# Two column blocks per bank in the output projections of a fused encoder trunk, and new planner estimates for two of its stages

## The chip, the cores and the metric

The kernel runs as one program on one core of a Trainium2 chip. The metric is the device time of one execution in microseconds (us). Where the profile gives instruction times and waits, they come from one profiled execution of the same program.

## The reference, cut to what matters

The kernel computes two layers of an encoder on one sequence of 256 positions (`S`) with 1024 features. Everything is float32. Each layer is a half feed-forward network, a mixer, a cross-attention to a memory of 256 positions, and another half feed-forward network; every one of them adds its result to `x`.

```python
for layer in range(2):
    x = x + 0.5 * swiglu(rms_norm(x, ...), ...)
    h = rms_norm(x, mix_norm[layer])
    if layer % 2 == 0:      # the "AB" mixer: differential attention | stick-breaking attention
        x = x + concat([from_heads(oa), from_heads(ob)]) @ w_out          # (256 x 1024) @ (1024 x 1024)
    else:                   # the "MLA" mixer: latent attention, 16 heads
        x = x + from_heads(o) @ w_o                                       # (256 x 1024) @ (1024 x 1024)
    x = x + memory_cross_attention(rms_norm(x, ...), rms_norm(mem, ...), ...)
                            # 4 heads of 128; its last step is (256 x 512) @ (512 x 1024)
    x = x + 0.5 * swiglu(rms_norm(x, ...), ...)
```

The three products written out above, the AB one, the MLA one and that of each cross-attention, are the output projections that the change is about. There are four of them in the program.

## The kernel before, in words

`x` is kept transposed: eight blocks of 128 features by 256 positions, called `dt` 0 to 7 here as in the code (d0 to d7 for short). Each product in full precision is made of three matmuls (`mm3`, L285 to L287): high part of the weight with high part of the data, then the low part of the data, then the low part of the weight. L287 is the one that reads the weight's low part in an output projection.

A weight chunk of 2048 columns comes by DMA into a raw buffer `wr` and is split there: ScalarE (ACT) copies it into `wh` (L250), and VectorE (DVE) subtracts that from the raw one into `wl` (L252). In the mixers and cross-attentions this goes in four quarters of 512 columns, and GpSimd (POOL) makes the last quarter of `wl`; in the two small projections of the cross-attentions some chunks go in eight pieces of 256. There are two raw buffers and three pairs of `wh` and `wl` (`HL = 3`). So the fourth chunk in a row can't be split before the last matmul that reads the first chunk.

An output projection is `out_g` (L654 to L684). Its source is in groups: four groups of two rows of 128 features in the mixers, in the order in which attention delivers them. Its weights are `nchunk` chunks, four with two column blocks each in the mixers, two with four blocks each in the cross-attentions. It goes by windows: the first is d0, d1 and d2 together, each with a PSUM bank of its own, group after group; then d3 to d7 come one at a time, with all groups in a row. There are three banks with the tag `mm`.

When a block's last group is done, `finish_dt` handles it. DVE adds the bank to `x` (L511); ACT makes the high part of the scaled block for the next stage (L482), DVE its low part (L483). These three are scheduled with high priority. ACT squares the block (L523), into `acc` for the first and into one of two buffers `sq` for the others, and POOL adds each square to `acc` (L531): seven additions in a row. After the first 48 matmuls of the next stage, TensorE (PE) sums `acc` over the partitions (L476), which starts the next norm.

TensorE's order is fixed by hand. In each stage a small planner (`run`, L438) holds a list of tasks with a priority each, and steps through them by an estimated clock: each step says which events, weights and banks it needs, and the tables `EST_X0`, `EST_X1`, `EST_AB` and `EST_MLA` tell after how many us an event of a task counts as done. The task that is ready, by these estimates, and has the best priority comes next. A weight counts as ready 4.41 us after the buffer it needs comes free. The order on the other engines is set afterwards by the framework's scheduler, from the program order, its own costs and the priorities. On the chip each engine then works its list strictly in that order.

In the AB stage the planner mixes attention with other work: `po` (L1105) is the product of stick-breaking weights and values, scores of the differential attention start at L323 and use two banks `s`, and the values of that part are multiplied at L1191. Beside them stand projections of the memory for the coming cross-attention; the keys of the memory are normalised on DVE (L853) and then transposed on PE (`transpose4`, L793), and `mem_k` is the task that does so, with a latency in its `yield` (L854).

Of the kernel before, what the change touches and what calls it, by code (L numbers as in the profile page):

```python
# [19 lines left out]
P = 128  # L20
S = 256
# [30 lines left out]
BANKS = {"mm": 3, "s": 2, "t": 2, "o": 1}  # L52
# [4 lines left out]
KRAW = True  # L57
PREADD = True

EST_X0 = {'scale': 3.59, 'rq': 1.14, 'psd': 1.46, 'sp': 2.8, 'p1': 4.06, 'p2': 0, 'o': 1.32, 'src': 8.83}  # L60
EST_X1 = {'scale': 2.31, 'rq': 1.14, 'psd': 1.46, 'sp': 2.8, 'p1': 3.39, 'p2': 0.0, 'o': 1.18, 'src': 8.83}
EST_AB = {'b': 1.33, 'va': 1.47, 'rot': 14.92, 'st1': 6.44, 'st2': 0.14, 'z': 1.55, 'sto': 2.4, 'src': 0.79, 'T': 0.74, 'sp': 3.0, 'pc': 8.7, 'pcT': 1.4, 'po': 4.35, 'oa': 8.7, 'srco': 1.25}
PRIO_MLA = [1, 2, 4.2, 3.9, 4.4, 2.3]
PRIO_AB = [1, 6.1, 4.1, 6.9, 6.9, 0.5]
EST_MLA = {'latd': 1.52, 'scale': 11.0, 'r': 1.8, 'kr': 4.06, 'pk': 2.4, 'pv': 1.23, 'v': 1.73, 'k': 6.43, 'kT': 0.9, 'q': 7.82, 'qT': 2.38, 'cs': 3.11, 'sp': 6.25, 'p1': 3.36, 'p2': 0.68, 'p3': 0.75, 'o': 0.58, 'src': 0.8}
# [96 lines left out]
def trunk_kernel(ctx, tc, wflat, xT_d, xtok_d, memT_d, memtok_d, gains_d, rows_d, cst_d, out_d):  # L162
# [57 lines left out]
    offs, o = [], 0  # L220
# [63 lines left out]
    def mm3(out, a, b, first, last, **kw):  # L284
        PE.matmul(out, a[0], b[0], start=first, stop=False, **kw)  # L285
        PE.matmul(out, a[0], b[1], start=False, stop=False, **kw)  # L286
        PE.matmul(out, a[1], b[0], start=False, stop=last, **kw)  # L287
        spend(3 * 0.109 * b[0].shape[-1] / 256)
# [96 lines left out]
    class Event:  # L385
        t = None
# [5 lines left out]
    def spend(n):  # L392
        od.cost += n
# [8 lines left out]
    def drop(ps, dur):  # L402
        tag, i, _ = od.own.pop(id(ps))
        od.pend.append((lambda t, tag=tag, i=i: od.bank[tag].__setitem__(i, t), dur))
# [75 lines left out]
    def split(hi, lo, src, g):  # L480

        return (A.activation(hi, src, AF.Identity, scale=g),  # L482
                V.scalar_tensor_tensor(out=lo, in0=src, scalar=g, in1=hi.bitcast(F32), op0=ALU.mult,  # L483
                                       op1=ALU.subtract))
# [17 lines left out]
    def begin_phase():  # L502
        st.at = x_at.pop(0)
        st.nxt = [None] * KT
        st.acc = None

    def finish_dt(dt, gc, ps=None, factor=1.0):
        xd = x[:, dt, :]
        if ps is not None:
            with tc.high_priority():  # L510
                V.scalar_tensor_tensor(out=xd, in0=ps, scalar=factor, in1=xd, op0=ALU.mult, op1=ALU.add)  # L511
        if gc is None:
            nc.sync.dma_start(out_d[:, dt, :], xd)
            return
        h, l = (z[:, st.at + dt * S:st.at + dt * S + S] for z in parts)
        st.nxt[dt] = (h, l)
        if ps is None:
            return split(h, l, xd, gcol(gc + dt))
        with tc.high_priority():
            split(h, l, xd, gcol(gc + dt))  # L520

        def square(dst):
            A.activation(dst, xd, AF.Square)  # L523

        if st.acc is None:
            st.acc = T("acc", [P, S], 2)
            square(st.acc)
        else:
            sq = T("sq", [P, S], 2)
            square(sq)  # L530
            G.tensor_tensor(out=st.acc, in0=st.acc, in1=sq, op=ALU.add)  # L531
# [121 lines left out]

    def out_g(keyf, nchunk, groups, gc):  # L654

        begin_phase()
        per = KT // nchunk
        ws, left, pss = {}, {c: per for c in range(nchunk)}, {}

        def part(dt, g):  # L660
            _, src, rows_ = groups[g]
            w = ws[dt // per]
            j = dt % per
            for i, k in enumerate(rows_):
                mm3(pss[dt][:, 0:S], (w[0][:, k, j * P:(j + 1) * P], w[1][:, k, j * P:(j + 1) * P]),
                    src[i], g == 0 and i == 0, g == len(groups) - 1 and i == len(rows_) - 1)
            if g == len(groups) - 1:
                left[dt // per] -= 1
                if not left[dt // per]:
                    done(keyf(dt // per))  # L670
                ps = pss.pop(dt)
                finish_dt(dt, gc, ps[:, 0:S])
                drop(ps, 0.8)

        nw = BANKS["mm"]
        for win in [tuple(range(nw))] + [(dt,) for dt in range(nw, KT)]:
            for g, (ev, _, _) in enumerate(groups):
                for dt in win:
                    yield dict(after=[ev], w=keyf(dt // per), mm=int(g == 0))
                    if dt // per not in ws:  # L680
                        ws[dt // per] = weight(keyf(dt // per), per * P)
                    if g == 0:
                        pss[dt] = take("mm")
                    part(dt, g)  # L684

# [149 lines left out]
    def mem_k(l, c, events):  # L835

        ps = yield from tm_g((f"memk{l}", c), memstate["x"])
        rm = memstate["rs"]

        def norm():  # L840
            yield dict(after=events)
            k = al()
            for t in range(2):
                A.activation(k[:, t * S:(t + 1) * S], ps[:, t * S:(t + 1) * S], AF.Identity, scale=rm[:, t:t + 1])
            drop(ps, 1.2)
            sq = al()
            G.tensor_tensor(out=sq, in0=k, in1=k, op=ALU.mult)
            v = sm()[:, 0:4]
            V.tensor_reduce(out=v, in_=sq.rearrange("p (a b) -> p a b", b=P), axis=AX.X, op=ALU.add)
            V.tensor_scalar(out=v, in0=v, scalar1=1.0 / P, scalar2=EPS, op0=ALU.mult, op1=ALU.add)  # L850
            r = rsqrt(v, 4)
            k3 = k.rearrange("p (a b) -> p a b", b=P)
            V.tensor_tensor(out=k3, in0=k3, in1=r.unsqueeze(2).to_broadcast([P, 4, P]), op=ALU.mult)  # L853
            yield dict(t=1, lat=7.0)  # L854
            pt = transpose4([k3[:, t * 2 + j, :] for j in range(2) for t in range(2)])
            kt = al()
            A.activation(kt, pt, AF.Identity, scale=gcol(G_XK + l))
            drop(pt, 0.9)
            rel(k, sq)
            memstate["k", l, c] = kt  # L860

        spawn(1, norm())
# [15 lines left out]
    def cross(l, gc):  # L878
        EST_X = (EST_X0, EST_X1)[l]
        xg = st.xg  # L880
# [89 lines left out]
    def mixer_ab(gc):  # L970
# [12 lines left out]
        def products():  # L983
            for key in ("qb", "kb"):
                for c in range(2):
# [5 lines left out]
                    def evac_b(key=key, c=c, ps=ps):  # L991
# [7 lines left out]
                        drop(ps, 0.9)  # L999
                        signal(ev[key, c], EST_AB['b'])  # L1000

                    spawn(0, after([ev["rb"]], evac_b))
            for key in AB_ORDER:
# [8 lines left out]
                for c in range(2):  # L1012
# [6 lines left out]
                    drop(ps, 1.2)  # L1019
                    signal(ev[key, c], EST_AB['va'])  # L1020
                if dst is None:
# [4 lines left out]
        def rotate(key):  # L1026
# [20 lines left out]
            if key == "qa":  # L1047
                rqs["r"] = r
            signal(ev[key], EST_AB['rot'])

# [9 lines left out]
        def stick(hq, g):  # L1060
# [25 lines left out]
            for i, (z, (sp, hh, hl)) in enumerate(zip(zs, sps)):  # L1086
                yield dict(lat=EST_AB['st2'] if i else EST_AB['st1'])
                for h_ in (hh, hl):
# [5 lines left out]
                strict(w_)  # L1094
                drop(z, EST_AB['z'])
                ws.append(w_)
                rel(sp, hh, hl)
            yield dict(lat=EST_AB['sto'], o=1 - g, after=[ev["vb", hq]] + [ev["po", hq]] * g)
            if g == 0:
# [504 lines left out]
```

## Time and profile before

| what | value |
|---|---|
| device time, median of three runs | 1088.73 us |
| the three runs | 1087.2, 1088.73, 1089.23 us |
| the profiled execution's own time | 1086.18 us |
| its span, first to last instruction | 1084.5 us |
| PE busy | 1063.0 us, 98 % of the span |
| DVE busy | 769.4 us, 71 % |
| ACT busy | 655.3 us, 60 % |
| POOL busy | 192.4 us, 18 % |
| share of PE in the chain that ended last | 90 % |
| HBM read | 190.79 MB |

A busy share is an average over the whole span. The chain that ended last is found backwards from the last instruction, at each step to what released it. The rows that follow further down come from four kinds of view: the page's summary, the sums of waits of an engine, an engine's instructions in order of time, and the busy time and granted TensorE clock of given stretches.

### The profile page before, as it was taken

To read this page: it belongs to the slowest core of one execution; us is meant where nothing else is said; L and a number is where in the kernel's file an instruction comes from. 1 tells how busy PE (TensorE), PEld (TensorE's weight loads), DVE (VectorE), ACT (ScalarE), POOL (GpSimd) and SP (SyncE) were. 2 spreads that over 40 slices of the span, in tenths; PEclk is the share of its full clock that TensorE was granted. 3 is DMA by queue.
4 is the path that set the end of the run, shared out by engine and by line. 5 is a ranking of instruction groups with operands and counts; after the bars stand their busy time and mean duration, and the time that the engine had idled before them with its cause. 6 is when DMAs were issued, how large, how long until landed. Compare 5 with 4: busy or idle time off the path is not lost.

```text
span 1084.5 us, 23380 instructions
## 1 busy us (share of the span) xinstructions
PE 1063.0 (98%) x9034; PEld 1044.5 (96%) x9034; DVE 769.4 (71%) x1866; ACT 655.3 (60%) x1775; POOL 192.4 (18%) x210
## 2 busy tenths in 40 slices
PE   8999999999899999999999999999989999999998
PEld 8999999998799999999999999999878999999998
DVE  5988765567867877776777777664688768777753
ACT  6766565567756665555666655565866567555542
POOL 0200001365434200000100000024861422000000
PEclk9999999999999999999999999999989999999999
DMA  8776556635345355555556565564341444555561
GB/s 285 247 250 218 197 191 206 195 89 184 99 136 195 119 193 196 193 185 199 200 189 220 200 208 184 182 197 158 97 147 49 155 150 164 195 195 195 185 225 58
DMA packets 51232, 193.36 MB, mean 178 GB/s; under 512 B 5808, under 2 KB 8368, under 8 KB 36016
## 3 DMA queue, kind: packets, MB, share of 16 engines
q1 hardware_dynamic: 50976, 191.81, 52.0%
q8 instruction: 71, 1.16, 0.4%
q14 instruction: 41, 0.34, 0.1%
q10 hardware_dynamic: 144, 0.05, 0.0%
HBM read 190.79 MB, written 1.05 MB: 177 GB/s over the span
## 4 chain that ended last, share of the span: by engine, by line
PE 90%; DVE 4%; ACT 2%; POOL 2%; issue 1%; DMA 1%; SPq 0%; DVEq 0%; ACTq 0%; POOLq 0%
PE mm L285 28%; PE mm L286 28%; PE mm L287 28%; DVE wl L252 1%; PE t L793 1%; ACT slotf L780 1%; POOL sm L468 1%; PE s L1448 1%; PE t L476 1%; DMA wr<-wflat 1%; PE s L918 0%; PE o L1481 0%; POOL sl L468 0%; PE s L285 0%; PE o L937 0%
## 5 line engine op out<-in xcount | busy, mean ns | idle before, releaser
L250 ACT CAST wh<-wr 128x256 fp32r<-128x256 f32 (+1 forms) x1216 | 441.0, 434 | 291.6 <-PE mm L286 234.2
L252 DVE TENSOR_TENSOR wl<-wr,wh 128x256 fp32r<-128x256 f32 (+1 forms) x1171 | 479.8, 466 | 125.6 <-ACT wh L250 120.2
L285 PE MATMUL mm<-xh,wh 128*128 128x256 f32 x1552 | 430.5, 277 | 1.9 <-ACT wh L271 1.9
L286 PE MATMUL mm<-xl,wh 128*128 128x256 f32 x1552 | 428.5, 276 | 0.0
L287 PE MATMUL mm<-xh,wl 128*128 128x256 f32 x1552 | 428.2, 276 | 0.0
L285 PEld LDWEIGHTS mm<-xh,wh 128*128 128x128 f32 x1552 | 292.3, 188 | 2.4 <-ACT wh L271 2.1
L286 PEld LDWEIGHTS mm<-xl,wh 128*128 128x128 f32 x1552 | 292.3, 188 | 0.6
L287 PEld LDWEIGHTS mm<-xh,wl 128*128 128x128 f32 x1552 | 292.1, 188 | 0.1
L285 PE MATMUL mm<-slotr,wh 128*128 128x256 f32 x896 | 247.6, 276 | 0.3 <-ACT slotr L482 0.3
L286 PE MATMUL mm<-slotr,wh 128*128 128x256 f32 x896 | 246.7, 275 | 0.4 <-DVE slotr L483 0.4
L287 PE MATMUL mm<-slotr,wl 128*128 128x256 f32 x896 | 246.6, 275 | 0.0
L285 PEld LDWEIGHTS mm<-slotr,wh 128*128 128x128 f32 x896 | 168.2, 188 | 1.0 <-ACT slotr L482 0.6
L286 PEld LDWEIGHTS mm<-slotr,wh 128*128 128x128 f32 x896 | 168.2, 188 | 0.7 <-DVE slotr L483 0.6
L287 PEld LDWEIGHTS mm<-slotr,wl 128*128 128x128 f32 x896 | 168.2, 188 | 0.0
L531 POOL TENSOR_TENSOR acc<-acc,sq 128x256 f32<-128x256 f32 x49 | 38.7, 789 | 452.5 <-ACT sq L523 450.4
L252 POOL TENSOR_TENSOR wl<-wr,wh 128x512 fp32r<-128x512 f32 x45 | 67.3, 1496 | 111.4 <-ACT wh L250 89.2
L739 DVE TENSOR_TENSOR slotf<-mm,rb 128x512 f32<-128x512 f32 x43 | 29.7, 690 | 53.7 <-PE mm L287 53.7
L482 ACT ACTIVATE xh<-x,gains 128x256 fp32r<-128x256 f32 x64 | 32.2, 507 | 27.8 <-DVE x L511 25.8
L780 ACT ACTIVATE slotf<-s,sm,sl 128x256 f32<-128x256 f32 (+1 forms) x64 | 32.7, 521 | 23.1 <-DVE sm L774 17.5
L729 DVE TENSOR_TENSOR slotf<-mm,rb 128x512 f32<-128x512 f32 x43 | 29.6, 689 | 21.0 <-PE mm L287 21.0
L511 DVE SCALAR_TENSOR_TENSOR x<-mm,x 128x256 f32<-128x256 f32 x64 | 26.8, 419 | 23.5 <-PE mm L287 23.5
L483 DVE SCALAR_TENSOR_TENSOR xl<-x,gains,xh 128x256 fp32r<-128x256 f32 x64 | 37.6, 592 | 5.7 <-ACT xh L482 5.5
(204 smaller groups left out, 1196.3 us busy)
## 6 DMA issues: line engine op xcount, KB each, us to landing
wr<-wflat SPq DMA_DIRECT2D x118, 1024.0 KB, 4.9
wr<-wflat SPq DMA_DIRECT2D x179, 256.0 KB, 3.9
wr<-wflat SPq DMA_DIRECT2D x16, 768.0 KB, 4.3
slotf<-memT SPq DMA_DIRECT2D x8, 256.0 KB, 3.4
wr<-wflat SPq DMA_DIRECT2D x2, 512.0 KB, 7.4
slotf<-xtok SPq DMA_DIRECT2D x4, 256.0 KB, 7.1
slotf<-memtok SPq DMA_DIRECT2D x4, 256.0 KB, 4.0
out<-x SPq DMA_DIRECT2D x8, 128.0 KB, 2.0
```

Source lines behind the costliest of these rows:

```text
L250: A.copy(hi[:, a:b], raw[:, a:b])
L252: e.tensor_tensor(out=lo[:, a:b], in0=raw[:, a:b], in1=hi[:, a:b].bitcast(F32), op=ALU.subtract)
L285: PE.matmul(out, a[0], b[0], start=first, stop=False, **kw)
L286: PE.matmul(out, a[0], b[1], start=False, stop=False, **kw)
L287: PE.matmul(out, a[1], b[0], start=False, stop=last, **kw)
L482: return (A.activation(hi, src, AF.Identity, scale=g), V.scalar_tensor_tensor(out=lo, in0=src, scalar=g, in1=hi.bitcast(F32), op0=ALU.mult ...
L483: V.scalar_tensor_tensor(out=lo, in0=src, scalar=g, in1=hi.bitcast(F32), op0=ALU.mult, op1=ALU.subtract))
L511: V.scalar_tensor_tensor(out=xd, in0=ps, scalar=factor, in1=xd, op0=ALU.mult, op1=ALU.add)
L531: G.tensor_tensor(out=st.acc, in0=st.acc, in1=sq, op=ALU.add)
L729: V.tensor_tensor(out=t.rearrange("p (a b) -> p a b", b=S), in0=pg.rearrange("p (a b) -> p a b", b=S), in1=rbb, op=ALU.mult)
L739: V.tensor_tensor(out=u.rearrange("p (a b) -> p a b", b=S), in0=pu.rearrange("p (a b) -> p a b", b=S), in1=rbb, op=ALU.mult)
L780: A.activation(p[:, i * w:(i + 1) * w], sps[:, i * w:(i + 1) * w], AF.Exp, bias=nb[:, i:i + 1], scale=r, accum_out=sums[:, i:i + 1])
```

## The change

`out_g` gets another first window and another use of the banks, and three tables and one latency get new numbers. The number of matmuls is the same.

```diff
-EST_X0 = {..., 'o': 1.32, 'src': 8.83}
-EST_X1 = {..., 'o': 1.18, 'src': 8.83}
-EST_AB = {..., 'va': 1.47, ..., 'sp': 3.0, ..., 'srco': 1.25}
+EST_X0 = {..., 'o': 1.6, 'src': 2.0}
+EST_X1 = {..., 'o': 1.6, 'src': 2.0}
+EST_AB = {..., 'va': 2.8, ..., 'sp': 4.4, ..., 'srco': 2.2}
...
+        nw = 2 * BANKS["mm"]
+
+        def bank(dt):
+            return dt // 2 * 2 if dt < nw else dt
...
+            b = bank(dt)
+            c0 = (dt - b) * S
             for i, k in enumerate(rows_):
-                mm3(pss[dt][:, 0:S], (w[0][:, k, j * P:(j + 1) * P], w[1][:, k, j * P:(j + 1) * P]),
-                    src[i], g == 0 and i == 0, g == len(groups) - 1 and i == len(rows_) - 1)
+                mm3(pss[b][:, c0:c0 + S], (w[0][:, k, j * P:(j + 1) * P], w[1][:, k, j * P:(j + 1) * P]),
+                    src[i], g == i == 0 and dt == b, g == len(groups) - 1 and i == len(rows_) - 1,
+                    skip_group_check=dt < nw)
             if g == len(groups) - 1:
                 left[dt // per] -= 1
                 if not left[dt // per]:
                     done(keyf(dt // per))
-                ps = pss.pop(dt)
-                finish_dt(dt, gc, ps[:, 0:S])
-                drop(ps, 0.8)
-
-        nw = BANKS["mm"]
+                if dt >= nw or dt > b:
+                    for d in range(b, dt + 1):
+                        finish_dt(d, gc, pss[b][:, (d - b) * S:(d - b + 1) * S])
+                    drop(pss[b], 0.8)
...
-            yield dict(t=1, lat=7.0)
+            yield dict(t=1, lat=9.0 if l == 0 else 7.0)
```

The first window now holds six column blocks in the three banks: d0 and d1 share the first bank (call the pair A), d2 and d3 the second (B), d4 and d5 the third (C). A pair is finished by `finish_dt` when its second block has its last matmul. d6 and d7 come alone, as before. In the mixers A reads the first weight chunk, B the second, C the third, and d6 and d7 the fourth.

What this does to the order is shown at three places. Line numbers of the changed kernel are larger by ten from about L690 on. First, DVE in the AB output projection, of before, from the split of the last attention group to the addition of d7. `wl_4069` and `wl_4098` are chunks 2 and 3 of the projection's weights:

```order
L252 TENSOR_TENSOR wl_4069<-wr_4067,wh_4068 128x512 x3
L511 SCALAR_TENSOR_TENSOR x<-mm_4089,x 128x256
L483 SCALAR_TENSOR_TENSOR xl<-x,gains,xh 128x256
L511 SCALAR_TENSOR_TENSOR x<-mm_4111,x 128x256
L252 TENSOR_TENSOR wl_4098<-wr_4096,wh_4097 128x512
L483 SCALAR_TENSOR_TENSOR xl<-x,gains,xh 128x256 x2
L252 TENSOR_TENSOR wl_4098<-wr_4096,wh_4097 128x512 x2
L511 SCALAR_TENSOR_TENSOR x<-mm_4203,x 128x256
```

The same place in the changed kernel; `wl_4075` is chunk 3, and `mm_4060`, `mm_4088` and `mm_4138` are the banks of A, B and C:

```order
L252 TENSOR_TENSOR wl_4047<-wr_4045,wh_4046 128x512 x3
L511 SCALAR_TENSOR_TENSOR x<-mm_4060,x 128x256 x2
L252 TENSOR_TENSOR wl_4075<-wr_4073,wh_4074 128x512 x2
L511 SCALAR_TENSOR_TENSOR x<-mm_4088,x 128x256 x2
L483 SCALAR_TENSOR_TENSOR xl<-x,gains,xh 128x256
L511 SCALAR_TENSOR_TENSOR x<-mm_4138,x 128x256 x2
L483 SCALAR_TENSOR_TENSOR xl<-x,gains,xh 128x256 x5
L252 TENSOR_TENSOR wl_4075<-wr_4073,wh_4074 128x512
```

Before, the third quarter of chunk 3 (the last row with `wl_4098`) stands behind three additions and three low parts; now the last row, the third quarter of `wl_4075`, stands behind six of each.

Second, PE in the AB stage where the memory's keys are transposed, of before; `t_3995` and `t_4001` are two of these groups of four transposes, and `mm_3982` is a projection of the memory:

```order
L286 MATMUL mm_3982<-wl_3769,mem 128x256
L287 MATMUL mm_3982<-wh_3768,mem 128x256
L793 MATMUL t_3995<-cst,slotf_2658 128x128 x4
L793 MATMUL t_4001<-cst,slotf_2678 128x128 x4
L285 MATMUL mm_3982<-wh_3768,mem 128x256
```

And in the changed kernel, where the second group, now `t_4039`, stands at the end of that projection:

```order
L285 MATMUL mm_3982<-wh_3738,mem 128x256
L286 MATMUL mm_3982<-wl_3739,mem 128x256
L287 MATMUL mm_3982<-wh_3738,mem 128x256
L803 MATMUL t_4039<-cst,slotf_2675 128x128 x4
L285 MATMUL mm_4060<-slotr_2682,wh_3847 128x256
```

The second group of transposes comes 36 matmuls later, right ahead of the first matmul of pair A.

Third, ACT in the output projection of the first cross-attention, of before, from the high part of d0 to that of d4; `wh_4799` is the second weight of the feed-forward stage that follows, and L523 makes the squares:

```order
L482 ACTIVATE xh<-x,gains 128x256
L523 ACTIVATE acc_4753<-x 128x256
L482 ACTIVATE xh<-x,gains 128x256
L523 ACTIVATE sq_4764<-x 128x256
L482 ACTIVATE xh<-x,gains 128x256
L523 ACTIVATE sq_4776<-x 128x256
L250 CAST wh_4799<-wr_4798 128x256 x3
L482 ACTIVATE xh<-x,gains 128x256
L523 ACTIVATE sq_4795<-x 128x256
```

The same place in the changed kernel, from the high parts of d0 and d1 to the squares of d1 and d2; `wh_4747` is the same weight:

```order
L482 ACTIVATE xh<-x,gains 128x256 x2
L523 ACTIVATE acc_4794<-x 128x256
L250 CAST wh_4747<-wr_4746 128x256 x3
L482 ACTIVATE xh<-x,gains 128x256 x2
L250 CAST wh_4747<-wr_4746 128x256
L482 ACTIVATE xh<-x,gains 128x256 x2
L250 CAST wh_4747<-wr_4746 128x256 x2
L482 ACTIVATE xh<-x,gains 128x256
L250 CAST wh_4747<-wr_4746 128x256 x2
L523 ACTIVATE sq_4799<-x 128x256
L523 ACTIVATE sq_4817<-x 128x256
```

Before, each square stood right behind the high part of its block; now those of d1 and d2 stand behind the high part of d6 and all eight casts of the weight.

## Rows read from the trace of the kernel before

**Rows 1.** The page's summary: busy time by engine, and the chain that ended last.

```profile
PE 1063.0 (98%) x9034; PEld 1044.5 (96%) x9034; DVE 769.4 (71%) x1866; ACT 655.3 (60%) x1775; POOL 192.4 (18%) x210
...
PE 90%; DVE 4%; ACT 2%; POOL 2%; issue 1%; DMA 1%; SPq 0%; DVEq 0%; ACTq 0%; POOLq 0%
```

**Rows 2.** PE's waits, 243 to 312 us: total, times, longest (us).

```profile
PE t L793 <- DVE slotf L853: 2.3, 1, 2.3
PE s L323 <- ACT slotf L780: 1.9, 2, 1.0
PE o L1105 <- issue: 0.9, 1, 0.9
PE o L1105 <- ACT slotf L1017: 0.9, 1, 0.9
```

**Rows 3.** In order of time (start, duration, count): the AB projection's start, DVE, PE.

```profile
300.02 0.68 DVE L252 TENSOR_TENSOR wl<-wr,wh 128x512 fp32r<-128x512 f32 x1
...
304.10 0.36 PE L285 MATMUL mm<-slotr,wh 128*128 128x256 f32 x1
```

**Rows 4.** Stretches (start:end, length): busy time of engines, PE clock, DMA, GB/s.

```profile
356.79:367.97 11.18, 11.18 (x99) 11.15 (x98) 9.48 (x24) 8.10 (x23) 2.81 (x4) 1.00 0.26 95
842.88:866.37 23.49, 23.49 (x206) 23.37 (x205) 18.29 (x29) 15.01 (x33) 11.42 (x11) 1.00 0.49 157
```

**Rows 5.** DVE in order of time in the AB output projection.

```profile
314.14 0.42 DVE L511 SCALAR_TENSOR_TENSOR x<-mm,x 128x256 f32<-128x256 f32 x1 [0.26 <-PE mm L287]
314.48 0.48 DVE L483 SCALAR_TENSOR_TENSOR xl<-x,gains,xh 128x256 fp32r<-128x256 f32 x1
...
316.71 1.29 DVE L252 TENSOR_TENSOR wl<-wr,wh 128x512 fp32r<-128x512 f32 x2
...
321.31 2.98 DVE L252 TENSOR_TENSOR wl<-wr,wh 128x512 fp32r<-128x512 f32 x2 [0.71 <-ACT wh L250]
```

**Rows 6.** ACT, and one row of POOL, in the same stretch.

```profile
314.34 0.61 ACT L250 CAST wh<-wr 128x512 fp32r<-128x512 f32 x1
314.85 0.51 ACT L482 ACTIVATE xh<-x,gains 128x256 fp32r<-128x256 f32 x1
...
316.18 1.13 ACT L250 CAST wh<-wr 128x512 fp32r<-128x512 f32 x2
...
322.40 1.35 POOL L252 TENSOR_TENSOR wl<-wr,wh 128x512 fp32r<-128x512 f32 x1 [0.37 <-ACT wh L250]
```

**Rows 7.** DVE in the MLA output projection.

```profile
846.63 0.42 DVE L511 SCALAR_TENSOR_TENSOR x<-mm,x 128x256 f32<-128x256 f32 x1 [0.26 <-PE mm L287]
...
849.20 1.29 DVE L252 TENSOR_TENSOR wl<-wr,wh 128x512 fp32r<-128x512 f32 x2
```

**Rows 8.** End of the first cross-attention: POOL's additions, ACT, PE's column sum.

```profile
362.04 1.65 POOL L531 TENSOR_TENSOR acc<-acc,sq 128x256 f32<-128x256 f32 x2 [13.71 <-ACT sq L523]
...
371.24 0.41 ACT L523 ACTIVATE sq<-x 128x256 f32<-128x256 f32 x1
371.55 1.62 ACT L250 CAST wh<-wr 128x256 fp32r<-128x256 f32 x5
...
371.79 0.75 POOL L531 TENSOR_TENSOR acc<-acc,sq 128x256 f32<-128x256 f32 x1 [0.88 <-ACT sq L523]
...
373.56 0.50 PE L476 MATMUL t<-ones,acc 128*128 128x2 f32 x4
```

**Rows 9.** PE's waits over the whole span, two of them.

```profile
PE s L1448 <- DVE slotf L1435: 2.6, 1, 2.6
...
PE o L937 <- DVE slotf L801: 1.1, 2, 0.6
```

**Rows 10.** Stretches before and in the drop of PE's clock (columns as in rows 4).

```profile
785.00:790.90 5.90, 3.65 (x31) 3.34 (x29) 2.85 (x9) 3.00 (x7) 4.93 (x8) 1.00 0.49 162
790.90:797.73 6.83, 6.43 (x24) 5.87 (x25) 5.26 (x10) 3.16 (x12) 4.07 (x4) 0.50 0.51 169
```

More of the change, by code (lines that the diff above doesn't have):

```diff
@@ L58 @@
 PREADD = True
-EST_X0 = {'scale': 3.59, 'rq': 1.14, 'psd': 1.46, 'sp': 2.8, 'p1': 4.06, 'p2': 0, 'o': 1.32, 'src': 8.83}
-EST_X1 = {'scale': 2.31, 'rq': 1.14, 'psd': 1.46, 'sp': 2.8, 'p1': 3.39, 'p2': 0.0, 'o': 1.18, 'src': 8.83}
-EST_AB = {'b': 1.33, 'va': 1.47, 'rot': 14.92, 'st1': 6.44, 'st2': 0.14, 'z': 1.55, 'sto': 2.4, 'src': 0.79, 'T': 0.74, 'sp': 3.0, 'pc': 8.7, 'pcT': 1.4, 'po': 4.35, 'oa': 8.7, 'srco': 1.25}
+EST_X0 = {'scale': 3.59, 'rq': 1.14, 'psd': 1.46, 'sp': 2.8, 'p1': 4.06, 'p2': 0, 'o': 1.6, 'src': 2.0}
+EST_X1 = {'scale': 2.31, 'rq': 1.14, 'psd': 1.46, 'sp': 2.8, 'p1': 3.39, 'p2': 0.0, 'o': 1.6, 'src': 2.0}
+EST_AB = {'b': 1.33, 'va': 2.8, 'rot': 14.92, 'st1': 6.44, 'st2': 0.14, 'z': 1.55, 'sto': 2.4, 'src': 0.79, 'T': 0.74, 'sp': 4.4, 'pc': 8.7, 'pcT': 1.4, 'po': 4.35, 'oa': 8.7, 'srco': 2.2}
 PRIO_MLA = [1, 2, 4.2, 3.9, 4.4, 2.3]
@@ L678, in out_g @@
                 for dt in win:
-                    yield dict(after=[ev], w=keyf(dt // per), mm=int(g == 0))
+                    yield dict(after=[ev], w=keyf(dt // per), mm=int(g == 0 and dt == bank(dt)))
                     if dt // per not in ws:
                         ws[dt // per] = weight(keyf(dt // per), per * P)
-                    if g == 0:
+                    if g == 0 and dt == bank(dt):
                         pss[dt] = take("mm")
```

## The prediction

> **What bounds the kernel now.** I read the summary first: the reader is to see that PE is busy for 98 % of the span and holds 90 % of the chain that ended last [rows 1]. So an edit counts only where it adds or removes idle time of PE, or changes PE's clock. The matmuls stay the same in number, so their own time drops out. The sums of PE's waits come second: the AB stage holds four kinds of wait that the new estimates can touch, each about 1 to 2 us long [rows 2]. Third come the stretches of the projections themselves: in the cross one 99 matmul records fill 11.18 of 11.18 us, in the MLA one 206 fill all 23.49, both at clock 1.00 [rows 4]. Nothing waits there, so the new window has nothing to win inside a projection. One matmul of 256 columns takes 23.49/206 = 0.114 us there, so 6 take 0.68, 12 take 1.37, 24 take 2.74 and 48 take 5.47. Last come DVE, ACT and POOL in order of time around the projections [rows 5 to 8].
>
> **The estimates in the AB stage.** Four waits are moved. The product at L1105 waited 0.9 for ACT's copy at L1017; 24 matmuls stand ahead of it now instead of 12, and 12 more last 1.37, so the wait goes: −0.9. The second L1105 wait, 0.9, is again behind that ACT queue, which other work of ACT fills, so I take half: −0.45. Scores at L323 waited twice for the softmax that holds their banks, 1.9 together, and are put 12 to 36 matmuls later: −1.9. The transposes at L793 waited 2.3 for DVE's L853; 36 matmuls, 4.1 us, now stand ahead: −2.3. Sum −5.55 [rows 2]. ScalarE's wait at the split of the last group is untouched.
>
> What is late next: PE comes to the projection sooner. It started at 304.10 before [rows 3]. By 5.55 us of waits, and some 1.2 us of attention work that now stands behind pair A's start, it would start at about 297.3, and the third matmul of pair B, 14 matmuls on, wants the low part of chunk 1 at about 299.0. DVE finished that at 300.02 + 0.68 = 300.70 [rows 3], behind a softmax chain that does not get shorter. That is a new wait of 1.7 if DVE's list keeps its times, none if DVE moves with PE; I take 1.7, and −3.85 for the stage (bounds −5.6 and −2.5, the latter if the second L1105 and one L323 keep their waits).
>
> **d6 in the AB projection.** This is the largest term. Chunk 3 can't be split until pair A's last matmul lets chunk 0 go. Before, d3, d4 and d5 then gave PE 3 × 2.74 = 8.2 us of work; now only the last groups of B and C stand between, 24 matmuls, 2.74. I set zero at DVE's first addition for A, about 0.35 us after A's last matmul. d6's third matmul, the first that reads `wl`, comes at 2.74 + 0.23 − 0.35 = 2.6, and in AB its group reads the third quarter. DVE's list to that quarter, from the order and the steps of [rows 5] (0.34 from one addition's start to the next row's, 0.40 for a low part, 0.60 to 0.68 for a quarter) and ACT's of [rows 6] (0.52 a cast, 0.41 to 0.51 a high part): two additions to 0.76; two quarters behind ACT's casts to 1.95; two additions to 2.7; one low part to 3.1; two additions to 3.85; then five low parts, for which ACT has made the last high part by 5.45 (two casts, two high parts, two casts, two high parts, one cast, two high parts from zero), to 5.85; the quarter itself to 6.5. So PE waits 6.5 − 2.6 = 3.9. From the other side: before, with three blocks finishing, the third quarter was done at 316.71 + 1.29 = 318.0, 3.9 after the addition at 314.14 [rows 5]; at that lag the wait is 3.9 − 2.6 = 1.3. Above, POOL can stretch the quarter: the two quarters at 321.31 took 2.98 us instead of the 1.29 of those at 316.71 [rows 5], while POOL's quarter of 1.35 ran at 322.40 [rows 6], which is 1.7 more. I take +4.2, near the worked-out list, with bounds 1.3 and 5.6.
>
> The Trainium skill ("SBUF — State Buffer", section on the two separate sides of SBUF) says that GpSimd and VectorE share one pair of SBUF ports, held by one instruction at a time while the other is blocked. The row of 2.98 us agrees with that; the rival on POOL below is what the rule would make of this place.
>
> **d6 in the MLA projection.** The list is the same, but there the groups read the quarters in order, so the third is wanted 12 matmuls later: 4.2 − 1.37 = +2.8. The lag before was 849.20 + 1.29 − 846.63 = 3.9 [rows 7], by which the wait would be none; bounds 0 and 4.2.
>
> **The column sum after the cross-attentions.** Both weight chunks fit there, so d6 does not wait. But the squares come late. Let b be the end of A's last group. d6 and d7 end at b + 2.74 + 2.74, and the 48 matmuls of the next stage at b + 11.0; there L476 wants `acc`. ACT's list puts d1's square behind seven high parts, the first square and eight casts: 7 × 0.41 + 0.31 + 8 × 0.32 = 5.7 us of work (a square and a cast by [rows 8]), begun at b + 0.8 and held by d6's addition, so d1's square is done at about b + 7. POOL's seven additions follow at 0.74 to 0.82 each [rows 8], 5.5 us: b + 12.4, so L476 is late by 1.4. Before, the last addition ended at 372.54 and L476 started at 373.56 [rows 8], so 1.0 of cover is gone as well. Bounds 0 and 2.5, taken +1.4, in both cross-attentions. In the MLA stage and in AB the wait at d6 gives POOL that time: 0.
>
> **The attention of the cross stages.** The smaller `src` puts the first matmuls of d0 before the last transposes; 18 matmuls then stand ahead of L937. In the second cross-attention its 0.6 wait [rows 9] goes: −0.6. In the first, the eight pieces of a weight now stand ahead of DVE's copy, so L937 waits as before: 0 (bounds −0.6 and +1). Two blocks in one bank cost nothing in PE's time, and the bank comes free with its second addition, earlier than d6 asks for it.
>
> **The sum.** −3.85 + 4.2 + 2.8 + 1.4 + 1.4 − 0.6 = +5.35. The profiled execution took 1086.18; the changed kernel's like run would take 1091.5. The median lies 2.55 above the profiled time, so I add the sum to it: 1088.73 + 5.35 = 1094.1.
>
> **The rivals.**
> *Faster: the splits come in time.* DVE and ACT are quicker than their lists suggest and chunk 3 has the lag of before, 3.9: d6 costs 1.3 in AB and nothing in MLA; the sums are in time; B finds its weight. −5.55 + 1.3 − 0.6 = −4.85, so 1083.9. For it speaks that this lag was measured twice [rows 5, 7]; against it, that it was with three blocks ahead, not six. It decides from a lag below about 4.5.
> *No change.* The lag of before at d6, but B's wait and the late sums come: −3.85 + 1.3 + 2.8 − 0.6 = −0.35, so 1088.4.
> *Slower still: the clock.* After 2.6 us of idle PE [rows 9] the clock stood at 0.50 (1.2 GHz) for 6.83 us [rows 10], which costs half of that, 3.4. The 2.3 us of L793 [rows 2] brought no drop. A wait of 4.2 at d6 is longer than either; if one drop follows, 1097.5, if two, 1100.9. Against it: two idle gaps of like length went different ways, so what decides is not seen here. The Trainium skill ("TensorE: Matmul & The Clock Gate", section on why this matters for kernels) warns of a fall to the half clock after idle gaps between bursts of matmuls; the drop above agrees, the wait without one shows that not every gap does it.
> *Slower still: POOL holds DVE up.* The fourth quarter on POOL blocks the low parts at both d6 for the 1.7 of the 2.98 row instead of the 0.3 that I took: 2 × 1.4, so 1096.9.
>
> **Chances.** Forecast 0.46, splits in time 0.18, no change 0.16, clock 0.10, POOL 0.10. A measurement of this kernel can tell 0.2 %, 2.2 us, from no change. Slower: 0.46 + 0.10 + 0.10 = 0.66; within: 0.16; faster: 0.18. The forecast's own range is 1091 to 1097. The range for 8 in 10 leaves out the fast half of the first rival and the second drop of the clock: 1085.0 to 1100.5.
>
> **What would show it.** In the profile after, PE's waits should hold L287 in `mm<-slotr,wl` waiting for DVE's L252 twice, some 4 and 3 us, at d6 of the two mixers, and L476 waiting for POOL's L531 twice, about 1.4. L793 for L853 and L1105 for L1017 should be gone, with a wait of 1 to 2 at pair B. If d6 starts without a wait, the main term is wrong: then DVE's list did not hold the third quarter back, and the first rival is right. If the clock row is below 1.00 right behind d6, the clock rival is. If the AB stage keeps its waits, the estimates did not move what stood late.

## The result, and the profile after

The changed kernel takes 1102.55 us (median of four runs, 1101.61 to 1104.08), the kernel before, on the same chip, 1088.36. The ratio is 1.0132, with a 95 % interval of 1.0115 to 1.015: about 14 us slower. The profiled execution took 1102.58 us, with a span of 1100.8, against 1086.18 and 1084.5 before: 16.3 us more. The direction was forecast, the size was not: +5.35 stood in the sum, and 1102.55 lies outside the range.

Where the time came in is read best from the start of L476, the column sum with which each projection's stage is handed on, in both traces:

| stretch | before | after | added in this stretch |
|---|---|---|---|
| AB, to its column sum | 333.88 | 338.86 | +4.98 |
| first cross-attention, to its column sum | 373.56 | 380.94 | +2.40 |
| the next 48 matmuls (end at L557) | 379.49 | 388.60 | +1.73 |
| feed-forward, MLA up to its last L1481 (L1491 after) | 841.43 | 850.23 | -0.31 |
| MLA, to its column sum | 866.37 | 880.63 | +5.46 |
| second cross-attention, to its column sum | 905.78 | 921.99 | +1.95 |
| to the end of the span | 1084.5 | 1100.8 | +0.1 |

The summary of the changed kernel, as in [rows 1]:

```profile
PE 1069.5 (97%) x9034; PEld 1049.5 (95%) x9034; DVE 771.2 (70%) x1866; ACT 656.2 (60%) x1775; POOL 192.3 (17%) x210
...
PE 81%; ACT 6%; DVE 5%; POOL 4%; issue 3%; DMA 1%; SPq 0%; DVEq 0%; POOLq 0%; ACTq 0%
```

The engines work as long as before, but PE's share of the chain that ended last fell from 90 to 81 %, and ACT, DVE and POOL together rose from 8 to 15 %. PE's waits over the whole span (total, times, longest):

```profile
PE mm L287 <- DVE wl L252: 9.6, 4, 3.9
PE t L476 <- POOL acc L531: 3.6, 2, 1.8
...
PE mm L286 <- DVE xl L483: 1.2, 2, 0.8
...
PE s L323 <- ACT slotf L790: 0.4, 1, 0.4
```

The waits of [rows 2] are gone or small. In their place stand four waits of L287 for the low part of a weight: at d6 in AB 3.9 and in MLA 2.6, and at pairs B and C in AB 2.6 and 0.6. The wait at d6 in MLA is this one:

```profile
868.38 0.38 PE L287 MATMUL mm<-slotr,wl 128*128 128x256 f32 x1 [2.56 <-DVE wl L252]
```

The two late column sums are there too, 1.8 each. PE around d6 in AB, in order of time:

```profile
320.93 0.28 PE L286 MATMUL mm<-slotr,wh 128*128 128x256 f32 x1
325.10 0.58 PE L287 MATMUL mm<-slotr,wl 128*128 128x256 f32 x1 [3.89 <-DVE wl L252]
325.48 0.41 PE L285 MATMUL mm<-slotr,wh 128*128 128x256 f32 x1
```

d6's third matmul waits 3.89 us, and the ones behind it last 0.41 instead of 0.28. DVE meanwhile, the list that the order showed:

```profile
318.26 0.76 DVE L511 SCALAR_TENSOR_TENSOR x<-mm,x 128x256 f32<-128x256 f32 x2 [5.08 <-PE mm L287]
318.93 1.29 DVE L252 TENSOR_TENSOR wl<-wr,wh 128x512 fp32r<-128x512 f32 x2
320.13 0.75 DVE L511 SCALAR_TENSOR_TENSOR x<-mm,x 128x256 f32<-128x256 f32 x2
320.80 0.48 DVE L483 SCALAR_TENSOR_TENSOR xl<-x,gains,xh 128x256 fp32r<-128x256 f32 x1
321.19 0.75 DVE L511 SCALAR_TENSOR_TENSOR x<-mm,x 128x256 f32<-128x256 f32 x2
321.85 2.59 DVE L483 SCALAR_TENSOR_TENSOR xl<-x,gains,xh 128x256 fp32r<-128x256 f32 x5
324.37 2.48 DVE L252 TENSOR_TENSOR wl<-wr,wh 128x512 fp32r<-128x512 f32 x4
```

The third quarter is the first of the four in the last row. It is done at about 325.0, 6.8 after the first addition; 6.5 was worked out. ACT and POOL behind it:

```profile
324.76 0.41 ACT L523 ACTIVATE acc<-x 128x256 f32<-128x256 f32 x1
325.07 0.70 ACT L523 ACTIVATE sq<-x 128x256 f32<-128x256 f32 x2
328.70 0.42 ACT L523 ACTIVATE sq<-x 128x256 f32<-128x256 f32 x1 [2.92 <-POOL acc L531]
...
330.64 2.17 ACT L250 CAST wh<-wr 128x512 fp32r<-128x512 f32 x4
```

```profile
321.31 1.27 POOL L252 TENSOR_TENSOR wl<-wr,wh 128x512 fp32r<-128x512 f32 x1 [14.45 <-ACT wh L250]
324.98 3.00 POOL L252 TENSOR_TENSOR wl<-wr,wh 128x512 fp32r<-128x512 f32 x1 [2.40 <-ACT wh L250]
327.95 3.98 POOL L531 TENSOR_TENSOR acc<-acc,sq 128x256 f32<-128x256 f32 x5
```

Here is what the prediction did not price. With two buffers for the squares ACT stands still until POOL has added, and POOL comes to its additions only at 327.95. The casts of a later weight wait behind these squares until 330.64, DVE's splits of it wait for the casts, and the low parts of d6 and d7 stand behind those splits. POOL's quarter took 3.00 us while DVE ran its four in 2.48; the quarter before it, at 321.31, took 1.27. That agrees with what the Trainium skill ("SBUF — State Buffer", section on the two separate sides of SBUF) says of the port pair that only one of the two can hold.

The clock, in stretches as in [rows 10], but with PE's busy time alone:

```profile
323.35:330.18 6.83, 5.08 (x24) 0.50 0.55 171
381.38:384.79 3.41, 3.41 (x18) 0.50 0.71 250
869.48:872.89 3.41, 3.41 (x18) 0.50 0.93 279
```

PE ran at half clock behind d6 in AB, behind the first late column sum, and behind d6 in MLA, but not behind the second column sum, which waited as long. At half clock a matmul starts every 0.21 us instead of every 0.11. The first cross-attention's end, ACT, POOL and PE:

```profile
374.32 0.72 ACT L523 ACTIVATE sq<-x 128x256 f32<-128x256 f32 x2
...
374.81 6.07 POOL L531 TENSOR_TENSOR acc<-acc,sq 128x256 f32<-128x256 f32 x7 [21.50 <-ACT sq L523]
...
380.94 0.64 PE L476 MATMUL t<-ones,acc 128*128 128x2 f32 x4 [1.80 <-POOL acc L531]
```

All seven additions run in one piece, begun 12.8 us later than the first of [rows 8] (5.0 of that is AB's delay), and L476 waits for the last.

### The profile page after: what moved, and what is told of

The parts are those of the page before. It is cut to its first block, busy times and chain, and to the rows that moved or that the text cites. A ratio compares the mean times of both kernels' runs of the same rounds, so it can differ in the third digit from the quotient of the medians.

```text
span 1100.8 us, 23376 instructions
## 1 busy us (share of the span) xinstructions
PE 1069.5 (97%) x9034; PEld 1049.5 (95%) x9034; DVE 771.2 (70%) x1866; ACT 656.2 (60%) x1775; POOL 192.3 (17%) x210
## 4 chain that ended last, share of the span: by engine, by line
PE 81%; ACT 6%; DVE 5%; POOL 4%; issue 3%; DMA 1%; SPq 0%; DVEq 0%; POOLq 0%; ACTq 0%
PE mm L285 25%; PE mm L286 25%; PE mm L287 25%; ACT wh L250 2%; DVE wl L252 2%; POOL acc L531 1%; ACT slotf L790 1%; POOL sm L468 1%; PE t L803 1%; ACT xh L482 1%; DMA wr<-wflat 1%; POOL wl L252 1%; PE s L1458 1%; PE t L476 1%; PE s L928 1%
## 5 line engine op out<-in xcount | busy, mean ns | idle before, releaser
L252 DVE TENSOR_TENSOR wl<-wr,wh 128x256 fp32r<-128x256 f32 (+1 forms) x1171 | 485.0, 473 | 128.6 <-ACT wh L250 123.5
L287 PE MATMUL mm<-xh,wl 128*128 128x256 f32 x1552 | 428.9, 276 | 0.0
L287 PEld LDWEIGHTS mm<-xh,wl 128*128 128x128 f32 x1552 | 292.9, 189 | 0.1
L287 PE MATMUL mm<-slotr,wl 128*128 128x256 f32 x896 | 249.1, 278 | 9.6 <-DVE wl L252 9.6
L287 PEld LDWEIGHTS mm<-slotr,wl 128*128 128x128 f32 x896 | 170.1, 190 | 10.4 <-DVE wl L252 10.4
L286 PEld LDWEIGHTS mm<-slotr,wh 128*128 128x128 f32 x896 | 170.1, 190 | 1.5 <-DVE slotr L488 0.8
L285 PEld LDWEIGHTS mm<-slotr,wh 128*128 128x128 f32 x896 | 170.1, 190 | 1.1 <-ACT slotr L482 0.6
L511 DVE SCALAR_TENSOR_TENSOR x<-mm,x 128x256 f32<-128x256 f32 x64 | 25.8, 420 | 33.6 <-PE mm L287 33.6
L483 DVE SCALAR_TENSOR_TENSOR xl<-x,gains,xh 128x256 fp32r<-128x256 f32 x64 | 34.0, 552 | 7.1 <-ACT xh L482 6.9
```

The lines of the kernel that those rows point to most:

```text
L252: e.tensor_tensor(out=lo[:, a:b], in0=raw[:, a:b], in1=hi[:, a:b].bitcast(F32), op=ALU.subtract)
```

## The experiments

Each run stands beside runs of the kernel before on its own chip, with medians from 1086.41 to 1087.45 instead of the 1088.36 above. So ratios compare better than times; the changed kernel has 1.0132.

**What each half of the change costs.** The first run has the new tables and latency with the old `out_g`, the second the new `out_g` with the old tables.

```diff
 e1_estimates: EST_X0, EST_X1, EST_AB and mem_k's lat as changed; out_g as before
 e2_outg:      out_g as changed; EST_X0, EST_X1, EST_AB and mem_k's lat as before
```

> The new estimates alone, with the output projections of before. Theory A (the loss is all in the projections: two waits at d6, late column sums, and half clock after them): the AB stage keeps the gain of its interior, some 5.9 us of idle PE gone against about 2.7 of new wait at d2, and no wait at d6: 1088.4 - 3 to - 4, about 1085. Rival B (the new order of the AB and cross stages is itself part of the loss): 1090 or more.

> The new windows alone, with the estimates of before. Theory A: the two waits at d6 (about 4.0 and 2.7 us), the half clock after them (2.3 and 1.7), waits for low parts of 1 to 1.7 in the MLA stage and the late column sums (about 2 each) all stay: 1088.4 + 13 to + 16, so 1101 to 1104. Rival B (the windows cost little by themselves and lose only together with the new order): below 1096.

The estimates alone took 1090.03 against 1086.89, ratio 1.0026 (1.0016 to 1.0037): slower, where I expected 1085. Theory A was wrong in its gain, and rival B's 1090 or more came. The new windows alone took 1104.9, ratio 1.0172 (1.015 to 1.0195): 18 us more than before, just above the 13 to 16 that I expected, and far from rival B. So the windows lose about 18 us, the estimates 3 with the old windows, and with the new windows the estimates seem to win 2 to 4 back (2.4 by the times, 4 by the ratios, whose intervals touch). In AB, the waits of the run with the estimates alone, 243 to 312 us:

```profile
PE t L793 <- DVE slotf L1202: 1.9, 1, 1.9
PE mm L285 <- ACT slotf L872: 1.5, 1, 1.5
PE mm L287 <- DVE wl L252: 0.8, 1, 0.8
```

The old waits are gone, and the last group of attention is late instead: PE stands 1.9 at its transposes for L1202. PE's idle time inside the stage had been cover for that chain. The next two runs split the estimates.

```diff
 e6_est_x:  only EST_X0 and EST_X1 as changed
 e7_est_ab: only EST_AB and mem_k's lat as changed
```

> The kernel before with the two tables of the cross-attentions changed alone. Theory A2 (from the run with all estimates: the smaller src puts the first matmuls of d0 to d2 ahead of the time at which ACT and DVE have split their source, and PE waits for L487, L488 and L937 there): + 2.5 in the first and + 0.9 in the second, 1086.9 + 3.4, about 1090.3. Rival (the loss of the run with all estimates is from AB): 1086 to 1088.

> The kernel before with EST_AB and the latency of mem_k changed alone. Theory A2 (the idle time inside the AB stage only covers the chain of the last attention group, so taking it away brings new waits of like length at d2 and at the last transposes): the same within 1 us, 1086 to 1088, with the waits for L853 and L780 gone and new ones for L252 at d2 and for L1202 at L793. Rival (the gain of the interior is real and the loss is the cross tables' alone): 1083 to 1084.5.

Both came as expected. The cross tables alone: 1090.41 against 1087.45, ratio 1.0029 (1.0019 to 1.0038). The AB table with mem_k: 1087.29, ratio 0.9997 (0.9987 to 1.0006). PE's waits in the first cross-attention with the cross tables alone, 340 to 380 us, show the price of an `src` that promises the split source too early:

```profile
PE mm L286 <- DVE slotr L488: 0.9, 2, 0.6
PE mm L285 <- ACT slotr L487: 0.7, 1, 0.7
PE o L937 <- DVE slotf L801: 0.6, 1, 0.6
```

**The windows, mixers and cross-attentions apart.**

```diff
 e3_window4 (on the changed kernel)
-        nw = 2 * BANKS["mm"]
+        nw = 2 * BANKS["mm"] - (2 if nchunk == 4 else 0)
 e5_cross_only (on the kernel before, with the new out_g)
+        pair = nchunk == 2
+        nw = BANKS["mm"] * (2 if pair else 1)
```

> The changed kernel with a first window of four blocks in two banks in the two mixers, so that d4 and d5 come alone again ahead of chunk 3; two blocks still share a bank, and the cross-attentions are as changed. Theory A: no wait at d6 and no half clock after it, 7 us back in AB and 5 in MLA: about 1090. Rival C (sharing a bank, with both blocks finished at once, is what costs): little comes back, 1098 or more.

> The kernel before with the new windows in the two cross-attentions alone (old windows in the mixers, old estimates). Theory A (each cross-attention loses by its late column sum, and half clock may follow): two waits of about 1.8 at L476 for POOL's additions, 3.6 in all, plus 0 to 3.2 for half clock behind them: 1086.9 + 3.6 to + 6.8, so 1090.5 to 1093.7, and no wait at the mixers' d6. Rival C (the loss is the mixers' alone): 1086 to 1088.

With a window of four, the waits at d6 are gone, and 1096.77 remains, ratio 1.008 (1.0058 to 1.0102): some 6 us back, not 12. A wait of 1.1 for L483 stands behind d6, and half clock follows it, in both mixers. So two blocks in a bank are not what makes PE wait at d6, and rival C's 1098 or more did not come; but theory A was not whole either. The cross-attentions alone: 1092.23 against 1087.45, ratio 1.0046 (1.0029 to 1.0062), with both waits of 1.8 at L476, inside what I expected.

**The column sum.**

```diff
 e8_squares (on the changed kernel; early is set in the cross-attentions)
         def square(dst):
-            A.activation(dst, xd, AF.Square)
+            with tc.high_priority() if early else nullcontext():
+                A.activation(dst, xd, AF.Square)
```

> The changed kernel with the squares of the cross-attentions' output projections scheduled with high priority, so that each stands right behind the high part of its block on ACT. Theory A (the column sum is late because ACT's list holds the squares back behind the casts of the next weight): the waits of 1.8 at L476 go, with the half clock behind the first: - 3.6 to - 5.2, so 1097.3 to 1099; the casts behind the squares may bring back up to 2. Rival E (POOL's seven serial additions are too slow anyway): the waits stay, 1102 to 1103.

1097.62 against 1087.45, ratio 1.0094 (1.0079 to 1.0109), as theory A expected. L476 no longer waits:

```profile
379.26 0.50 PE L476 MATMUL t<-ones,acc 128*128 128x2 f32 x4
```

From the first finished block, 368.58, to this start are 10.68 us; the changed kernel has 12.65 (368.29 to 380.94). POOL's additions are fast enough once the squares come in time; rival E falls.

**Filling the wait at d6.**

```diff
 e4_filler (on the changed kernel)
+                    if nchunk == 4 and dt == nw and g == 0:
+                        fill, f0 = take("s"), groups[0][1][0][0]
+                        many = 34 if groups[0][2][0] == 4 else 22
+                        for n in range(many):
+                            PE.matmul(fill[:, 0:S], f0[:, 0:P], f0, start=n == 0, stop=n == many - 1)
...
```

> The changed kernel with matmuls that compute nothing of use ahead of d6 in the two mixers, 34 in AB and 22 in MLA, about as long as the waits there; nothing is left out. Theory A with the clock (a fall to half clock follows the idle gap): the wait becomes work of the same length, the clock stays at 1.00, and the kernel gets faster although PE does more: 2 to 4 us, about 1099.5. Rival D (the half clock there has nothing to do with the idle gap, or comes on its own): same time or up to 2 us slower, 1102.5 to 1104.5.

1106.62, ratio 1.0184 (1.0161 to 1.0207): slower, a clear miss. d6 no longer waits, and the clock holds right behind it. But PE then reaches the next stage early and stands there, in order of time:

```profile
336.07 0.39 PE L286 MATMUL mm<-xl,wh 128*128 128x256 f32 x1 [0.85 <-DVE xl L483]
...
338.68 0.48 PE L286 MATMUL mm<-xl,wh 128*128 128x256 f32 x1 [1.34 <-DVE xl L483]
```

Half clock then follows these waits instead, in AB and in MLA:

```profile
338.81:345.64 6.83, 6.83 (x33) 0.50 0.75 243
884.94:891.77 6.83, 6.83 (x32) 0.50 0.82 268
```

That costs more than behind d6, for here PE has work all the time: 33 and 32 matmuls instead of 24 and 18. It is most of why the span here, 1108.1, is longer than the changed kernel's 1100.8. So in the changed kernel the half clock behind d6 ran, for the most part, inside time that PE would have waited in anyway. Removing the order at d6 instead tells the same:

```diff
 e9_lowlate (on the changed kernel; late is set for d0 to d5 in the mixers)
+        if late:
+            split(h, l, xd, gcol(gc + dt))
+        else:
+            with tc.high_priority():
+                split(h, l, xd, gcol(gc + dt))
```

> The changed kernel with the high and low parts of d0 to d5 scheduled without high priority in the two mixers; DVE's list then has the third quarter of chunk 3 ahead of all low parts. Theory A (the waits at d6 are DVE's order): the third quarter is done 3.3 us after the first addition of pair A instead of 6.8, so the wait at d6 falls from 3.9 to 0.5 to 1.5 in AB and to nothing in the MLA stage, with no half clock after them; low parts that come later may cost up to 2 at the next stage: 1102.5 - 6 to - 9, so 1093.5 to 1096.5. Rival (the release of the buffer or ACT's casts set the wait): 1100 or more, with the waits in place.

The wait at d6 fell to 1.2, just as worked out from DVE's list, and was gone in MLA. But the time was 1101.91 against 1086.41, ratio 1.0143 (1.0127 to 1.0158): nothing came back, a miss. DVE's quarter moved up, and the column sum became late in the mixers as well (2.1 in MLA):

```profile
321.98 1.54 DVE L252 TENSOR_TENSOR wl<-wr,wh 128x512 fp32r<-128x512 f32 x1
...
323.58 0.39 PE L287 MATMUL mm<-slotr,wl 128*128 128x256 f32 x1 [1.23 <-DVE wl L252]
...
338.48 0.61 PE L476 MATMUL t<-ones,acc 128*128 128x2 f32 x4 [2.54 <-POOL acc L534]
```

**What stands behind the wait.** Four buffers for the squares instead of two, without and with the filler:

```diff
 e10_sq4, e11_sq4_filler
-            sq = T("sq", [P, S], 2)
+            sq = T("sq", [P, S], 4)
```

> The changed kernel with four buffers for the squares instead of two. Theory F (behind d6 the end of the mixers is set by ACT, whose squares wait for POOL's additions and hold the casts and the low parts of d6 and d7 back; the half clock runs inside that time): ACT's squares no longer wait 2.9 us, the waits for L483 at the next stage go, but PE at half clock takes their place: 0 to - 2.5, so 1100 to 1102.5. Rival G (nothing but the half clock sets that stretch): no change at all, and no change in the next run against this one's partner without the buffers.

> The run before it in this list with the 34 and 22 matmuls of no use ahead of d6 as well. Theory F: with the clock at 1.00 and the squares no longer in the way, the time behind d6 shrinks: 2 to 4 us less than with four buffers alone, 1097 to 1099.5. Rival G2 (what follows d6 is set by DVE and ACT whatever the buffers and the clock): no gain over four buffers alone, 1101 or more.

1102.49, ratio 1.0144 (1.013 to 1.0158), and 1103.82, ratio 1.0164 (1.015 to 1.0178). With four buffers the wait for L483 in AB goes (in MLA one of 1.3 stays) and the time is the same: PE at half clock fills it. That lies at the end of theory F's range, where rival G says the same. With the filler theory F missed, and rival G2's lack of a gain came: PE is at full clock behind d6 in AB, but waits 1.4 for L483, so four buffers don't free ACT enough. The last three runs take the squares and additions of d1 to d7 out of the mixers altogether:

```diff
 e13_noadds (on the changed kernel), e14_noadds_filler (on e4_filler), e15_noadds_lowlate (on e9_lowlate);
 plain is set in the mixers
-        else:
+        elif not plain:
             sq = T("sq", [P, S], 2)
```

> The changed kernel without the squares of d1 to d7 and POOL's seven additions in the two mixers' output projections; this leaves out seven eighths of the sum of squares for the norm behind them. Theory H (the end of a mixer has limits one behind the other: DVE's order at d6, then ACT and POOL, which the additions fill): the waits at d6 stay at 3.9 and about 2.6, the waits for L483 behind them go, the half clock stays; the time from the first finished block to the column sum falls from 20.6 and 19.1 to about 20 and 17.5: 1100.5 to 1102. Rival I (POOL's additions are what holds the third quarter back): the waits at d6 shrink by over 1 us each, below 1098.

> The same, with 34 and 22 matmuls of no use ahead of d6; it leaves out the same part. Theory H: with nothing behind d6 that waits for ACT and POOL, the clock counts: the filler keeps it at 1.00, and the time from first block to column sum is 2.74 + 3.9 + 5.5 + 5.6 = 17.7 to 18.3 in AB, 2 us less than without filler, and the kernel 2 to 3 us faster than without filler although PE does more. Rival D (the half clock costs nothing here): no gain, same as without filler or slower.

> The changed kernel with the high and low parts of d0 to d5 without high priority in the mixers and without the squares and additions there; it leaves out the same part as the two before. Theory H (both limits removed at once): the wait at d6 falls to about 1.2 in AB and 0 in MLA, none for L476 there, and the time from first block to column sum to 15 to 16.5 in both: 4 to 5 us back in AB and 3 to 4 in MLA, 1093 to 1096. Rival J (weights or the low parts themselves set the end): stays above 18, 1099 or more.

They took 1103.51 (ratio 1.0141, 1.0115 to 1.0166), 1099.0 (1.0116, 1.0096 to 1.0136) and 1095.56 (1.0084, 1.0069 to 1.0099), against 1086.52. The third came as theory H expected. The second is faster than the first by more than the 2 to 3 forecast, but the two intervals overlap; its AB stretch, 18.13 in the table, lies in the 17.7 to 18.3 forecast. The first lies above its range, with d6's waits unchanged, against rival I; its trace has half clock behind pair B and behind the second column sum, where the changed kernel's has none. Such drops ahead of or behind a stretch differ from run to run, so the stretches tell more than the times. Read from the traces, from the start of the first finished block's addition (L511) to the start of L476:

| kernel | AB | MLA |
|---|---|---|
| before | 20.42 | 20.41 |
| changed | 20.60 | 19.08 |
| e9: low parts after the weight | 19.03 | 19.00 |
| e10: four buffers | 20.15 | 18.00 |
| e11: four buffers, filler | 19.80 | 18.00 |
| e4: filler | 21.17 | 19.65 |
| e13: no additions | 20.32 | 16.27 |
| e14: no additions, filler | 18.13 | 16.26 |
| e15: no additions, low parts after the weight | 14.95 | 14.20 |

The ends of the AB stretch before, and in e15:

```profile
313.46 0.42 DVE L511 SCALAR_TENSOR_TENSOR x<-mm,x 128x256 f32<-128x256 f32 x1 [2.34 <-PE mm L287]
333.88 0.39 PE L476 MATMUL t<-ones,acc 128*128 128x2 f32 x3
```

```profile
318.04 0.76 DVE L511 SCALAR_TENSOR_TENSOR x<-mm,x 128x256 f32<-128x256 f32 x2 [5.07 <-PE mm L287]
332.99 0.50 PE L476 MATMUL t<-ones,acc 128*128 128x2 f32 x4
```

PE's own work in that stretch is 20.2 with the old windows (two last groups, five blocks of 24 and 48 matmuls: 1.4 + 13.7 + 5.5, less 0.35 at the start) and 13.3 with the new (2.7 + 5.5 + 5.5 - 0.35). Before, PE was the limit. In the changed kernel it is not: only with both limits removed, DVE's order at d6 and the additions, does the stretch come near PE's work. In MLA some of what e15 wins is lost again right behind it: the next column sum there waits 2.2 for ACT's L912, where the changed kernel waits 0.6 at the same place. The clock is the third: without additions, e13 (first) ran at half clock behind d6 in AB and e14 (second) did not, in stretches as above:

```profile
325.57:332.40 6.83, 5.71 (x27) 0.50 0.64 202
```

```profile
318.00:340.00 22.00, 21.85 (x189) 1.00 0.44 144
```

and that is 2.2 us in AB (20.32 against 18.13), none in MLA, where neither lost clock inside the stretch. With the additions in place the same clock is worth 0.35 in AB (e10 at half clock behind d6, e11 at full clock).

**A version that beats both.**

```diff
 e12_memk9 (on the kernel before)
-            yield dict(t=1, lat=7.0)
+            yield dict(t=1, lat=9.0 if l == 0 else 7.0)
```

> The kernel before with the latency of mem_k at 9.0 in the first layer alone. Theory A2: the 2.3 us in which PE waits at L793 for L853 are filled with 24 matmuls, and the last attention group (L1191, then L1202 and the last transposes) comes earlier by about 1, since nothing of it is put behind other work: 1086 to 1086.5 where before has 1087.4, too small to be sure of. Rival (a new wait of the same length, as with all of EST_AB): no change.

1084.29 against 1086.41, ratio 0.9979 (0.997 to 0.9988): a small gain, clear of the noise, and about twice what I expected. In the trace AB's column sum starts at 332.24 instead of 333.88, 1.6 sooner. Its waits in AB, 243 to 312 us, keep those of [rows 2] but the first:

```profile
PE s L323 <- ACT slotf L780: 1.9, 2, 1.0
PE o L1105 <- issue: 0.9, 1, 0.9
PE o L1105 <- ACT slotf L1017: 0.8, 1, 0.8
```

The 2.3 us for L853 went and nothing of that length took their place, since no attention work was put behind other work for it. The three other numbers of EST_AB take that gain away again (e7).

## Why the prediction was wrong

- **The waits in the AB interior** went as forecast: PE came to the first matmul of the projection at 296.09 instead of 304.10 [rows 3], 8.0 sooner, of which 2.15 is attention work that now stands behind it (the group of L1201 at 301.13, 1.79, and four transposes, 0.36): 5.9, against 5.55 forecast.
- **The new wait at pair B** was there, 2.6 instead of 1.7, and pair C added 0.6. The last two groups began 2.1 later than before, with 36 matmuls more behind them, 4.2 us. So 2.1 of the gain remained instead of 3.85. The first matmul of these groups, before and after:

```profile
309.73 0.38 PE L285 MATMUL mm<-slotr,wh 128*128 128x256 f32 x1 [0.34 <-ACT slotr L482]
```

```profile
311.79 0.38 PE L285 MATMUL mm<-slotr,wh 128*128 128x256 f32 x1 [0.34 <-ACT slotr L482]
```

- **d6 in AB**: forecast 4.2, measured 3.9. **d6 in MLA**: forecast 2.8, measured 2.6. DVE's list from the order, priced by rows of before, was right to 0.3 us. The rival with the lag of before fell. So did the one with POOL: its quarter of chunk 3, at 321.31, ran beside five low parts that took 2.59, only about 0.5 more than worked out for them.
- **The column sum after the cross-attentions**: forecast 1.4 each, measured 1.8 each. e8 shows the cause named: ACT's list. The 0.6 at L937 went in both, and a wait of 0.6 for L488 took its place in the first.
- **The step that failed** is the sum's treatment of what follows d6 in the two mixers. It took the waits, +4.2 and +2.8, as all that is lost there, and put the way on to the column sum at nothing ("In the MLA stage and in AB the wait at d6 gives POOL that time: 0"). For L476 alone that zero held: it waited for POOL in neither mixer. But behind the wait at d6, AB lost 3.0 more (27.07 us for the 168 matmuls from 311.79, less 19.5 of work, the wait of 4.05 and the 0.5 of the split that was there before) and MLA 2.7 (5.46 less 2.72 with restart). In the changed kernel's own trace this is half clock, about 2.3 (24 matmuls in 5.08 instead of 2.74) and 1.6 (16 started in 3.41 instead of 1.82), and waits for d7's low part with restart, about 0.5 and 1.0. The runs show what stood in that time: POOL's additions with ACT's squares, the low parts of d6 and d7 behind them, and half clock, each hidden by the other. Filler removes the idle gap and finds the low parts (e4); moving the quarter up finds the additions (e9); without additions the clock shows, 2.2 (e13, e14); without both the stretch falls to 15 and 14 us (e15).
- **The clock** was a rival at 0.10, priced at 3.4 a drop. By the sign that I had named, half clock right behind d6, it came true. The drop behind the first cross-attention's column sum cost 1.7 and was in no case of mine. Those behind d6 cost less than 3.4 each, 2.3 and 1.6, and mostly hid other waits. So that rival's time, 1100.9 for two drops, lies near the 1102.55 in part by luck.
- **In sum**: 5.35 forecast; 5.7 left out behind the two d6, 1.7 of half clock behind the first column sum, 1.7 too much gain in AB, 1.0 and 1.2 too little in the two cross-attentions make about 16.6. The two waits at d6, forecast 0.2 too long, and 0.3 less in the feed-forward stretch bring that to about 16.2, against 16.3 in the spans.

What stays open: why half clock follows one wait and not another of the same length. It is not the place in the program alone. Eleven of the traces have the wait of 1.8 at both L476 of the cross-attentions; half clock follows the first in seven of them and the second in four, and in the changed kernel's trace only the first.

## What to carry to other kernels

Pricing a new wait is not enough: ask when the first block is finished, and what the other engines must do from there to the hand-over, as a sum for each engine beside that of PE. Grouping more blocks in one window bunches that work; here it took the limit from PE (20 us of its own work) and gave it to DVE, ACT and POOL in turn. And when a removed wait gives nothing back (e4, e9), look for the next one in the same stretch before pricing either: here they didn't add up.

## What was not expected of the hardware

The same idle gap is not followed by the same clock: 1.80 us at L476 was followed by half clock at 381.38 and not at 921.99. The 2.3 us at L793 were not followed by it before, but the same wait in e6 was, at 297.29. The 2.6 us at pair B were not in the changed kernel, and were in seven of the ten traces that have this wait with the new tables. So one trace of a kernel doesn't tell whether a wait brings half clock. And half clock has no fixed price: behind d6 in AB it cost 2.2 us where nothing else limited PE (e13 against e14), and 0.35 where ACT and DVE's low parts were due later anyway (e10 against e11).
